# A token router run in batches of tiles behind its first stage, its rows stored from ACT's queue, and all eighteen weight chunks allowed early

## Chip, cores and metric

One core of one Trainium2 chip runs the whole program. The metric is the device time of one execution in microseconds (us). The program has two layers, and each ends in a mixture of experts (MoE) whose weights are streamed from HBM.

## The reference

Each layer normalises its tokens, runs four token mixers, projects their output with one 1024 x 1024 matrix, adds it to the stream with a gate, and then runs the MoE. Layer 0 has 768 tokens (512 latent, 256 context), the MoE of layer 1 only the 512 latent ones. The part around the change is this:

```
def moe_ffn(h, wg, bg, we, be, w_gate, w_up, w_down):
    lg = hf @ wg + bg                                  # 4 groups
    g_sel = argmax(lg); p_sel = softmax(lg)[g_sel]
    le_sel = (hf @ we + be).reshape(T, 4, 8)[g_sel]     # 8 experts of the group
    top_v, top_i = lax.top_k(le_sel, 2)
    wts = softmax(top_v) * p_sel
    ...
    y_e = (silu(x @ w_gate[e]) * (x @ w_up[e])) @ w_down[e]   # 32 experts, 1024 -> 512 -> 1024
    out[token] += wts * y_e
```

h is the normalised and modulated stream: x times its inverse root mean square (rs), times one row of factors, plus one row of offsets. Latent and context tokens have different rows.

## The kernel before

Tokens lie on partitions, 128 to a tile: 6 tiles in layer 0, 4 in layer 1. A scheduler orders the instructions of each engine by program order among those that it takes to be ready; what it has ordered, an engine runs strictly in turn.

**Output projection and first stage.** The last part of the projection (`c == 3`) makes a quarter of the columns of every tile: 24 matmuls on TensorE (PE, L1787), a product on VectorE (DVE, L1790) and an addition to `x1[t]` on GpSimd (POOL, L1791). `token_tile(t)` follows two tiles behind (`LAG = 2`): `x1[t]` is stored to `acc` (L1753), eight transposes go to PSUM (L1757), ScalarE (ACT) squares the tile and sums it (`row_rs`, L1170) and copies the transposes back (L1759), sixteen matmul passes give 36 logits (L1762). DVE makes rs by a Newton iteration (`small_rsqrt`, L1154 to L1162), the product of the row h2 (L1768), POOL adds the offsets (L1769), and h2 is stored to DRAM (L1770). For tiles 0 and 4 the two modulation rows and the gain are loaded and multiplied (L1764 to L1766); tile 4 is the first context tile and reuses their buffers. All these transfers are issued by SyncE's queue (SP). The buffer `h2` exists twice and also holds the gain.

**Router.** `rt.tile(t)` runs one tile behind that: three rounds of `first_max` (L891 to L894), softmax parts, two small matmuls that rank the tokens of an expert (L922, L923), the values EV (L932), the slots S (L936) and matmuls into the tables L (L937). `finish` turns L into gather and scatter indices (`table`, L956 to L970) and the counts of each expert.

**Weights.** An expert's weights are six chunks of 1 MB. There are 18 chunk slots, so three experts fit. `fetch(n)` issues the loads of chunks up to n on SP; at most five are on their way (`FLIGHT`), and a load waits until its slot is free. Four chunks (layer 0) or seven (layer 1) are loaded before the last part of the projection. The other slots lie over the projection's operands (freed by its last matmul) and over `x1` and the router's buffers. After the router `fetch(FIRST[l])` allows chunks up to 12 in layer 0 and 16 in layer 1; those up to 18 wait until the second gather has landed (L1109). A later chunk waits for PE to have read the chunk that lies in its slot.

**Experts.** POOL gathers an expert's tokens by index (L990), PE transposes them (L1000) and multiplies gate and up (L1012), then the hidden part is transposed (L1025) and multiplied down (L1039), and POOL adds the rows to `acc` by index (L1052). An expert with more than 64 tokens takes a second round.

## Time and profile before

| | us |
|---|---|
| median of 3 runs (lowest, highest) | 2423.11 (2415.92, 2425.83) |
| the profiled execution | 2419.79 |
| its span, first to last instruction | 2418.0 |
| layer 0: last projection matmuls start / first gather issued / first expert's transposes | 771.35 / 812.19 / 818.01 |
| layer 1: first stage of tile 1 on PE / first gather issued / first expert's transposes | 1873.32 / 1911.46 / 1916.62 |

The mean granted clock of PE is 0.956 of 2.4 GHz. Layer 0's experts lie in the long stretch of about 400 GB/s in the first half of the page, layer 1's in the one that ends the program. In a timeline a row is: start, duration, engine, line, operation, tiles, count, and in brackets the engine's idle time before it with what ended it. SPq is SP's queue, where a transfer's issue stands, not its landing. Times in a timeline are us from the first instruction; "mean" in a group by line is in ns.

### The profile page before, as it was taken

To read this page: it belongs to the slowest core of one execution; us is meant where nothing else is said; L and a number is where in the kernel's file an instruction comes from. 1 tells how busy PE (TensorE), PEld (TensorE's weight loads), DVE (VectorE), ACT (ScalarE), POOL (GpSimd) and SP (SyncE) were. 2 spreads that over 40 slices of the span, in tenths; PEclk is the share of its full clock that TensorE was granted. 3 is DMA by queue.
4 is the path that set the end of the run, shared out by engine and by line. 5 is a ranking of instruction groups with operands and counts; after the bars stand their busy time and mean duration, and the time that the engine had idled before them with its cause. 6 is when DMAs were issued, how large, how long until landed. Compare 5 with 4: busy or idle time off the path is not lost. (4 is left out here: it accounts for less than half of the span.)

```text
span 2418.0 us, 32200 instructions
## 1 busy us (share of the span) xinstructions
PE 2039.0 (84%) x11540; PEld 1186.2 (49%) x11540; DVE 999.4 (41%) x2435; ACT 573.2 (24%) x1138; POOL 537.2 (22%) x429
## 2 busy tenths in 40 slices
PE   5789999999999598887777598999899598877775
PEld 1458778766688333322222386686669333222221
DVE  6751865537746522221112437645584511111110
ACT  4433431344622100000000234314352100000000
POOL 1653413211013122211111225131102221111111
PEclk9999999999998699999999799999999699999998
DMA  6434524202244899999999425420233899999996
GB/s 242 165 116 176 194 105 147 81 9 69 85 143 142 299 378 387 405 401 404 400 395 411 173 92 175 147 103 18 86 126 133 313 393 410 409 408 409 410 403 258
DMA packets 139311, 581.54 MB, mean 241 GB/s; under 512 B 23984, under 2 KB 47873, under 8 KB 88630
## 3 DMA queue, kind: packets, MB, share of 16 engines
q1 hardware_dynamic: 124054, 555.89, 59.5%
q0 software_dynamic: 15008, 22.36, 3.9%
q8 instruction: 152, 2.49, 0.4%
q14 instruction: 97, 0.79, 0.1%
HBM read 554.17 MB, written 36.80 MB: 244 GB/s over the span
## 5 line engine op out<-in xcount | busy, mean ns | idle before, releaser
L1012 PE MATMUL pb<-side,arena 128*64 128x512 f32 x1224 | 288.9, 604 | 45.9 <-DMA side<-in_w_moe 42.2
L1016 DVE COPY arena<-pb 128x512 f32<-128x512 f32 x67 | 46.3, 691 | 501.5 <-PE pb L1012 501.5
L1012 PE MATMUL pb<-arena 128*64 128x512 f32 x920 | 217.9, 605 | 41.8 <-DMA arena<-in_w_moe 38.2
L1028 ACT ACTIVATE arena<-pb 128x256 f32<-128x256 f32 x67 | 25.7, 383 | 902.9 <-PE pb L1025 902.9
L1276 POOL TENSOR_TENSOR wl<-side,wh 128x1024 fp32r<-128x1024 f32 x52 | 125.4, 2412 | 395.5 <-ACT wh L1275 267.1
L1012 PEld LDWEIGHTS pb<-side,arena 128*64 128x64 f32 x1224 | 81.4, 137 | 246.5 <-issue 126.4
L1300 PE MATMUL pw<-hh,wh 128*128 128x512 f32 (+1 forms) x720 | 168.6, 366 | 3.1 <-DVE arena L495 1.9
L1300 PE MATMUL pw<-hh,wl 128*128 128x512 f32 (+1 forms) x720 | 160.5, 358 | 0.0
L1043 DVE SCALAR_TENSOR_TENSOR arena<-pb,arena 128x512 f32<-128x512 f32 x67 | 50.3, 750 | 263.2 <-PE pb L1039 254.5
L1039 PE MATMUL pb<-side,arena 128*64 128x512 f32 x576 | 137.8, 617 | 24.9 <-DVE arena L1029 20.4
L1300 PE MATMUL pw<-hl,wh 128*128 128x512 f32 (+1 forms) x720 | 158.2, 355 | 0.0
L1012 PEld LDWEIGHTS pb<-arena 128*64 128x64 f32 x920 | 62.2, 138 | 190.8 <-issue 96.0
L1052 POOL DMA_INDIRECT acc<-arena x35 | 55.2, 1577 | 387.8 <-DVE arena L1047 338.5
L1300 PEld LDWEIGHTS pw<-hh,wh 128*128 128x128 f32 x720 | 117.8, 190 | 36.1 <-issue 14.4
L1039 PE MATMUL pb<-arena 128*64 128x512 f32 x496 | 115.5, 599 | 21.3 <-DVE arena L1029 20.8
L1300 PEld LDWEIGHTS pw<-hh,wl 128*128 128x128 f32 x720 | 117.9, 189 | 25.1 <-issue 9.9
L1300 PEld LDWEIGHTS pw<-hl,wh 128*128 128x128 f32 x720 | 117.4, 189 | 24.4 <-issue 8.7
L1052 POOL DMA_INDIRECT out_dram<-arena x32 | 50.9, 1590 | 311.4 <-DVE arena L1043 297.2
L990 POOL DMA_INDIRECT arena<-h2d,arena x67 | 69.8, 1042 | 187.5 <-issue 56.0
L1791 POOL TENSOR_TENSOR arena<-arena 128x256 f32<-128x256 f32 x40 | 31.2, 782 | 292.2 <-DVE arena L1790 278.2
L1025 PE MATMUL pb<-ident,arena 128*128 128x128 f32 x268 | 42.4, 280 | 55.4 <-DVE arena L1016 55.4
L1039 PEld LDWEIGHTS pb<-side,arena 128*64 128x64 f32 x576 | 39.0, 140 | 101.5 <-issue 60.8
(367 smaller groups left out, 3444.2 us busy)
## 6 DMA issues: line engine op xcount, KB each, us to landing
side<-in_w_moe SPq DMA_DIRECT2D x215, 1024.0 KB
arena<-in_w_moe SPq DMA_DIRECT2D x169, 1024.0 KB
arena<-in_w_ada SPq DMA_DIRECT2D x53, 512.0 KB
side<-in_w_in SPq DMA_DIRECT2D x52, 512.0 KB
side<-in_w_ada SPq DMA_DIRECT2D x43, 512.0 KB
arena<-in_w_out SPq DMA_DIRECT2D x16, 512.0 KB
arena<-in_x SPq DMA_DIRECT2D x12, 512.0 KB
spd<-arena SPq DMA_DIRECT2D x23, 256.0 KB
```

What stands on the lines that cost most here:

```text
L990: E.gathered = nc.gpsimd.indirect_dma_start(out=xg, out_offset=None, in_=h2d, in_offset=bass.IndirectOffsetOnAxis(ap=gi, axis=0), **(dict( ...
L1012: nc.tensor.matmul(pg[64 * s:64 * s + 64], xT[:, j // 4, j % 4, :], W[j // 2][:, (j % 2) * 1024 + s * 512:(j % 2) * 1024 + s * 512 + 512], ...
L1016: nc.vector.tensor_copy(gu, pg)
L1025: nc.tensor.transpose(pt[:, c * 128:(c + 1) * 128], gu[:, c * 128:(c + 1) * 128], E.c["ident"])
L1028: nc.scalar.activation(hT, pv[:, :, 0, :], AF.Silu)
L1039: nc.tensor.matmul(pd[64 * s:64 * s + 64], hT[:, c, :], W[4 + c // 2][:, (c % 2) * 1024 + s * 512:(c % 2) * 1024 + s * 512 + 512], start=( ...
L1043: nc.vector.scalar_tensor_tensor(y, pd, w[0], g2[0], op0=ALU.mult, op1=ALU.mult)
L1052: E.nc.gpsimd.indirect_dma_start(out=acc, out_offset=bass.IndirectOffsetOnAxis(ap=si, axis=0), in_=y, in_offset=None, compute_op=ALU.add, ...
L1276: (nc.vector if k % 2 else nc.gpsimd).tensor_sub(lo, src, hi.bitcast(F32))
L1300: nc.tensor.matmul(ps[:, :n], w[:, j, :], h[:, j, a:a + n], start=(i == 0), stop=(i == 23))
L1791: nc.gpsimd.tensor_add(x1[t][:, cc], x1[t][:, cc], tmp)
```

## The change

The work of a token tile is cut in two. `token_tile(t, i)` keeps what needs no VectorE: the store of `x1[t]`, transposes, square, copy and logits, which now gather in one PSUM tile and one rs tile for a batch. A batch is tiles 0 to 3, and in layer 0 also tiles 4 and 5 (`BATCHES`). When the first stage of all tiles has been written down, `token_batch` makes rs, logits, modulation rows and h2 for a whole batch, and `rt.tiles` routes it: one instruction for up to four tiles where there was one for each. Operations that took a number for each partition as an operand become operations on two tensors, one of them broadcast. `finish` makes both tables at once. The stores of `x1` and h2 and the loads of the gain and the modulation rows move from SP's queue to ACT's. `FIRST` becomes 18 in both layers, so no chunk waits for a gather. The arena grows by 128 columns.

```diff
-FIRST = (12, 16)
+FIRST = (18, 18)
+BATCHES = (((0, 4), (4, 2)), ((0, 4),))
     def first_max(self, v, w, iota, tag):
         nc.vector.reduce_max(m, v, axis=AX)
-        nc.vector.scalar_tensor_tensor(e, v, m, iota, op0=ALU.is_equal, op1=ALU.mult)
+        nc.vector.tensor_tensor(e, v, wide(m), op=ALU.is_equal)
+        nc.vector.tensor_tensor(e, e, row, op=ALU.mult)
         nc.vector.tensor_reduce(i, e, axis=AX, op=ALU.min)
-        nc.vector.tensor_scalar(e, iota, i, None, op0=ALU.is_equal)
+        nc.vector.tensor_tensor(e, row, wide(i), op=ALU.is_equal)
-    def tile(self, t, lg):
+    def tiles(self, t0, lg):
...
+        nc.vector.tensor_sub(sm[:, 0], v2, v1)
+        nc.scalar.activation(sm[:, 0], sm[:, 0], AF.Exp)
         nc.vector.tensor_add(Ab, E1, E2)
+        for i in range(n):
+            nc.vector.tensor_add(self.seen[:, t0 + i + 1], self.seen[:, t0 + i], Ab[:, i])
+            nc.tensor.matmul(rk[:, i], E.c["before_b"], Ab[:, i], start=True, stop=False, skip_group_check=True)
+            nc.tensor.matmul(rk[:, i], E.c["ones_b"], self.seen[:, t0 + i], start=False, stop=True, skip_group_check=True)
...
+            nc.vector.tensor_tensor(self.EV[:, k, tt], bcast(Ek.unsqueeze(2), P, n, 6, 32),
+                                    bcast(v[:, k].unsqueeze(3), P, n, 6, 32), op=ALU.mult)
+        for k, Ek in enumerate((E1, E2)):
+            nc.vector.tensor_tensor(Ek, Ek, rk, op=ALU.mult)
+            nc.vector.tensor_reduce(self.R[:, k, tt], Ek, axis=AX, op=ALU.add)
+        nc.vector.tensor_scalar(R1, self.R[:, :, tt], -float(NSLOT), None, op0=ALU.add)
+        for k in range(2):
+            for b, R in enumerate((self.R[:, :, tt], R1)):
+                nc.vector.tensor_tensor(S, bcast(self.slots.unsqueeze(1), P, n, 128),
+                                        bcast(R[:, k].unsqueeze(2), P, n, 128), op=ALU.is_equal)
+                for i in range(n):
+                    nc.tensor.matmul(self.L[:, b * 512:b * 512 + 192], S[:, i],
+                                     self.EV[:, k, t0 + i].rearrange("p v e -> p (v e)"),
+                                     start=(t0 + i == 0 and k == 0), stop=(t0 + i == self.nt - 1 and k == 1),
+                                     skip_group_check=True)
-            def token_tile(t):
-                nc.sync.dma_start(half_rows(acc[l], t), x1[t])
+            def token_tile(t, i):
+                nc.scalar.dma_start(half_rows(acc[l], t), x1[t])
...
-                rs = row_rs(E, x1[t], "rs2")
+                lg, rs = batch[t - i]
+                nc.scalar.activation(E.t("xoj", DM, BF16, bufs=1), x1[t], AF.Square, accum_out=rs[:, i:i + 1])
                 nc.scalar.copy(hTt, pt.rearrange("p (j t) -> p j t", j=8))
                 for j in range(8):
+                    nc.tensor.matmul(lg[:, i], hTt[:, j], wa[v][:, j], start=(j == 0), stop=(j == 7),
+                                     skip_group_check=True)
+            def token_batch(t0, n):
+                nc.vector.tensor_scalar(rs, rs, 1.0 / DM, EPS, op0=ALU.mult, op1=ALU.add)
+                small_rsqrt(E, rs, "rs2", n)
+                nc.vector.tensor_tensor(lg, ps, bcast(rs.unsqueeze(2), P, n, 36), op=ALU.mult)
+                nc.vector.tensor_tensor(lg, lg, bcast(cb[v].unsqueeze(1), P, n, 36), op=ALU.add)
+                if t0 % 4 == 0:
+                    n2 = E.load("h2", d[f"n2g{l}"], bufs=2, queue=nc.scalar)
+                    mod[:] = [bc_row(v, 4, "rsc", 1, nc.scalar), bc_row(v, 3, "rsh", 1, nc.scalar)]
+                    nc.vector.scalar_tensor_tensor(mod[0], mod[0], 1.0, n2, op0=ALU.add, op1=ALU.mult)
+                for i in range(n):
+                    h2 = E.t("h2", DM, bufs=2)
+                    nc.vector.scalar_tensor_tensor(h2, x1[t0 + i], rs[:, i:i + 1], mod[0], op0=ALU.mult, op1=ALU.mult)
+                    nc.gpsimd.tensor_add(h2, h2, mod[1])
+                    nc.scalar.dma_start(half_rows(h2d[l], t0 + i), h2)
+                rt.tiles(t0, lg)
                     if c == 3 and t >= LAG:
-                        logits.append(token_tile(t - LAG))
-                        if t > LAG:
-                            rt.tile(t - LAG - 1, logits[t - LAG - 1])
-            rt.tile(nt - 1, logits[-1])
+                        t0, n = [b for b in batches if b[0] <= t - LAG][-1]
+                        token_tile(t - LAG, t - LAG - t0)
+            for t0, n in batches:
+                token_batch(t0, n)
```

## Rows read from the trace of the kernel before

**Rows 1.** The page's head: span, and GB/s in 40 equal slices

```profile
span 2418.0 us, 32200 instructions
...
GB/s 242 165 116 176 194 105 147 81 9 69 85 143 142 299 378 387 405 401 404 400 395 411 173 92 175 147 103 18 86 126 133 313 393 410 409 408 409 410 403 258
```

**Rows 2.** Windows, layer 0: busy us (instructions) by engine, PE clock, DMA share, GB/s

```profile
780.00:800.00 20.00, 12.72 (x65) 11.96 (x65) 17.54 (x94) 4.33 (x10) 4.68 (x2) 0.50 0.58 205
...
900.00:920.00 20.00, 18.39 (x90) 6.51 (x88) 3.90 (x6) 0.97 (x2) 2.64 (x2) 1.00 0.98 371
920.00:940.00 20.00, 17.69 (x88) 6.56 (x86) 5.55 (x9) 1.94 (x4) 4.20 (x3) 1.00 0.97 375
```

**Rows 3.** SP's waits (total, times, longest): 880:920, 920:960, 1920:2000

```profile
SPq L1378 <- PE pb L1012: 8.1, 4, 4.3
...
SPq L1378 <- PE pb L1039: 10.4, 4, 5.4
...
SPq L1378 <- PE pb L1012: 11.6, 8, 5.3
```

**Rows 4.** Timeline of SP's queue, layer 0, router

```profile
772.48 0.33 SPq L1378 DMA_DIRECT2D side<-in_w_moe  x1
...
776.56 1.21 SPq L1511 DMA_DIRECT2D arena<-modd  x2
...
798.92 0.32 SPq L1770 DMA_DIRECT2D h2d<-arena  x1
```

**Rows 5.** Timeline of POOL, both layers

```profile
757.03 2.37 POOL L1769 TENSOR_TENSOR arena<-arena 128x1024 f32<-128x1024 f32 x1 [2.13 <-DVE arena L1768]
...
812.19 1.25 POOL L990 DMA_INDIRECT arena<-h2d,arena  x1 [13.30 <-DVE arena L948]
...
1911.46 1.07 POOL L990 DMA_INDIRECT arena<-h2d,arena  x1 [18.84 <-DVE arena L964]
...
1963.38 1.61 POOL L1052 DMA_INDIRECT out_dram<-arena  x1 [7.35 <-DVE arena L1043]
...
1976.28 1.60 POOL L1052 DMA_INDIRECT out_dram<-arena  x1 [7.16 <-DVE arena L1043]
```

**Rows 6.** Timeline of PE, both layers, from projection to first expert

```profile
771.35 1.11 PE L1787 MATMUL pw<-woh,ol 128*128 128x256 f32 x8
...
796.70 0.18 PE L922 MATMUL pb<-arena,before_b 128*128 128x32 bf16 x1 [6.76 <-DVE arena L919]
...
818.01 1.09 PE L1000 MATMUL pb<-ident,arena 128*128 128x128 f32 x4 [8.17 <-DMA arena<-h2d,arena]
...
1873.32 1.03 PE L1757 MATMUL pa<-ident,arena 128*128 128x128 f32 x8
...
1896.54 3.63 PE L1762 MATMUL pb<-arena 128*128 128x36 f32 x16 [1.10 <-ACT arena L1759]
...
1916.62 1.12 PE L1000 MATMUL pb<-ident,arena 128*128 128x128 f32 x4 [7.45 <-DMA arena<-h2d,arena]
```

**Rows 7.** Groups by line (busy, mean ns, idle before), DVE and ACT, 745:815

```profile
L892 DVE SCALAR_TENSOR_TENSOR arena<-arena,miota 128x32 f32<-128x32 f32 (+1 forms) x18 | 9.1, 509 | 0.1
L1768 DVE SCALAR_TENSOR_TENSOR arena<-arena 128x1024 f32<-128x1024 f32 x6 | 7.7, 1280 | 0.2
...
L1790 DVE TENSOR_TENSOR arena<-pw,arena 128x256 f32<-128x256 f32 x6 | 2.5, 416 | 2.5 <-PE pw L1787 2.5
...
L1759 ACT COPY arena<-pa 128x1024 f32<-128x1024 f32 x6 | 6.0, 1005 | 5.3 <-PE pb L1762 3.9 <-PE pa L1757 1.3
```

**Rows 8.** Timeline of DVE, layer 0: beside a POOL addition, and two chained steps

```profile
757.35 2.07 DVE L892 SCALAR_TENSOR_TENSOR arena<-arena,miota 128x4 f32<-128x4 f32 x1
...
806.10 0.25 DVE L892 SCALAR_TENSOR_TENSOR arena<-arena,miota 128x32 f32<-128x32 f32 x1
806.38 0.19 DVE L893 TENSOR_REDUCE arena<-arena 128x1 f32<-128x32 f32 x1
```

**Rows 9.** The gathers' line: issue to landing, all 67 of both layers

```profile
DMA to landing us min/median/max: 3.6/7.5/10.4
```

More of the change, by code (lines that the diff above doesn't have):

```diff
@@ L886, in first_max @@
     def first_max(self, v, w, iota, tag):
-        E, nc = self.E, self.E.nc
-        m, i = E.t(tag + "m", 1, bufs=2), E.t(tag + "i", 1, bufs=2)
-        e = E.t(tag + "e", w, bufs=2)
+        E, nc, n = self.E, self.E.nc, v.shape[1]
+        m, i = E.t(tag + "m", 4, bufs=1)[:, :n], E.t(tag + "i", 4, bufs=1)[:, :n]
+        e = E.t(tag + "e", [4, w], bufs=1)[:, :n]
+        wide = lambda a: bcast(a.unsqueeze(2), P, n, w)
+        row = bcast(iota.unsqueeze(1), P, n, w)
         nc.vector.reduce_max(m, v, axis=AX)
-        nc.vector.scalar_tensor_tensor(e, v, m, iota, op0=ALU.is_equal, op1=ALU.mult)
+        nc.vector.tensor_tensor(e, v, wide(m), op=ALU.is_equal)
@@ L921, in tile @@
-        rk = E.p1()[:, :32]
-        nc.tensor.matmul(rk, E.c["before_b"], Ab, start=True, stop=False, skip_group_check=True)
-        nc.tensor.matmul(rk, E.c["ones_b"], self.seen[:, t], start=False, stop=True, skip_group_check=True)
-        v = self.vals[:, :, t]
+        nc.vector.tensor_sub(sm[:, 0], v2, v1)
+        nc.scalar.activation(sm[:, 0], sm[:, 0], AF.Exp)
+        Ab = E.t("rA", [4, 32], BF16, bufs=1)[:, :n]
+        nc.vector.tensor_add(Ab, E1, E2)
+        rk = E.p1()[:, :n * 32].rearrange("p (n e) -> p n e", e=32)
@@ L925, in tile @@
+        w = sm[:, 2:4]
+        nc.vector.reciprocal(w[:, 0], sm[:, 1])
+        nc.vector.tensor_mul(w[:, 1], w[:, 0], sm[:, 0])
+        v = self.vals[:, :, tt]
         for part in range(3):
-            nc.vector.tensor_copy(v[:, :, 2 + part], w)
+            nc.vector.tensor_copy(v[:, :, :, 2 + part], w)
             if part < 2:
-                nc.vector.tensor_sub(w, w, v[:, :, 2 + part])
-        tmp = E.t("rtmp", 32, bufs=2)
+                nc.vector.tensor_sub(w, w, v[:, :, :, 2 + part])
@@ L930, in tile @@
         for k, Ek in enumerate((E1, E2)):
-            R, EV = self.R[:, k, t:t + 1], self.EV[:, k, t]
-            nc.vector.tensor_tensor(EV, bcast(Ek.unsqueeze(1), P, 6, 32), bcast(v[:, k].unsqueeze(2), P, 6, 32), op=ALU.mult)
-            nc.vector.tensor_tensor_reduce(tmp, Ek, rk, 1.0, 0.0, op0=ALU.mult, op1=ALU.add, accum_out=R)
-            for b in range(2):
-                S = E.t("rS", 128, BF16, bufs=4)
-                nc.vector.tensor_scalar(S, self.slots, float(b * NSLOT), R, op0=ALU.add, op1=ALU.is_equal)
-                nc.tensor.matmul(self.L[:, b * 512:b * 512 + 192], S, EV.rearrange("p v e -> p (v e)"),
-                                 start=(t == 0 and k == 0), stop=(t == self.nt - 1 and k == 1), skip_group_check=True)
+            nc.vector.tensor_tensor(self.EV[:, k, tt], bcast(Ek.unsqueeze(2), P, n, 6, 32),
+                                    bcast(v[:, k].unsqueeze(3), P, n, 6, 32), op=ALU.mult)
@@ L940, in finish @@
     def finish(self):
         E, nc = self.E, self.E.nc
-        tables = [self.table(self.L[:, b * 512:b * 512 + 192], 32, self.keep, f"s{b}") for b in range(2)]
+        gi, si, w = self.table(self.L.rearrange("p (b c) -> p b c", b=2)[:, :, :192], 2, 32, self.keep, "s")
         c = E.p1()[:, :32]
@@ L1761, in token_tile @@
                 for j in range(8):
-                    nc.tensor.matmul(ps[:, :36], hTt[:, j], wa[v][:, j], start=(j == 0), stop=(j == 7))
-                if t % 4 == 0:
-                    n2 = E.load("h2", d[f"n2g{l}"], bufs=2)
-                    mod[:] = [bc_row(v, 4, "rsc", 1), bc_row(v, 3, "rsh", 1)]
-                    nc.vector.scalar_tensor_tensor(mod[0], mod[0], 1.0, n2, op0=ALU.add, op1=ALU.mult)
-                h2 = E.t("h2", DM, bufs=2)
-                nc.vector.scalar_tensor_tensor(h2, x1[t], rs, mod[0], op0=ALU.mult, op1=ALU.mult)
@@ L1769, in token_tile @@
[L1769 to L1775 removed]
+                    nc.tensor.matmul(lg[:, i], hTt[:, j], wa[v][:, j], start=(j == 0), stop=(j == 7),
+                                     skip_group_check=True)
+            def token_batch(t0, n):
+                v = t0 // 4
+                ps, rs = (a[:, :n] for a in batch[t0])
+                nc.vector.tensor_scalar(rs, rs, 1.0 / DM, EPS, op0=ALU.mult, op1=ALU.add)
+                small_rsqrt(E, rs, "rs2", n)
+                lg = E.t("rlg", [4, 36], bufs=1)[:, :n]
+                nc.vector.tensor_tensor(lg, ps, bcast(rs.unsqueeze(2), P, n, 36), op=ALU.mult)
[3 more added lines that the diff above has]
+                    mod[:] = [bc_row(v, 4, "rsc", 1, nc.scalar), bc_row(v, 3, "rsh", 1, nc.scalar)]
+                    nc.vector.scalar_tensor_tensor(mod[0], mod[0], 1.0, n2, op0=ALU.add, op1=ALU.mult)
+                for i in range(n):
[4 more added lines that the diff above has]
+                rt.tiles(t0, lg)
@@ L1776, in trunk @@
+            mod, batch = [], {}
+            batches = BATCHES[l]
             for c in range(4):
```

83 lines of the change are left out of this document (35 added, 48 removed).

## The prediction

> **What bounds the kernel now.** Read first the page's head: both expert stages run at about 400 GB/s, and the five slices before the first one rises, with attention, projection and router, lie at 9 to 143 [rows 1]. A chunk of 1 MB (1.049 MB in the page's unit) takes 1.049/0.405 = 2.6 us at such a rate, so an expert's six take 15.6 us of transfer. It is tempting to say that whatever fills the empty slices earlier comes off the end. The windows at the start of the experts speak against that: in layer 0 the share of the DMA engines is 0.98 and 0.97 and the rate 371 and 375 GB/s between 900 and 940 [rows 2], and SP's waits say why: there it waits for PE to have read a slot, 8.1 us in four waits, then 10.4 in four; in layer 1 11.6 us in eight [rows 3]. PE takes an expert in 1976.28 - 1963.38 = 12.9 us [rows 5], faster than the transfers, but it starts with three experts in the slots and everything behind them waits for it. So the transfers catch up with PE early in both layers, and what they were ahead before that is lost. From there the end moves with the moment at which PE starts the first expert, almost one for one: 818.01 and 1916.62 [rows 6].
>
> That moment is set by the router. The first gather is issued at 812.19 and 1911.46, in both layers after a long idle time of POOL that ended with the router's tables on DVE [rows 5]. In layer 0 DVE is busy 17.54 of 20 us with 94 instructions [rows 2], and PE stands 6.76 us in front of a ranking matmul that waits for DVE, with the logits of the last tile behind it [rows 6]. So I ask of each part of the change what it does to the two first gathers.
>
> **First stage.** No router matmul now stands between the tiles' first stages. On PE a tile's projection is 24 matmuls at 1.11/8 us less their overlap, some 2.9 us. Before, the last eight started at 771.35 and ended at 772.5 [rows 6]; without the router's waits I take some 767.5. A tile's first stage after that is transposes 1.03 (1.0), copy 1.0 [rows 6, 7] and logits of about half of the 3.63 us that they take at half clock, 1.9: 4 us, since one PSUM buffer makes them follow each other. Layer 0: the logits of tile 3 at 771.5, of tile 5 at 779.5. Layer 1: tile 1 starts at 1873.32, three tiles later it is 1885.3, or 1889.6 if the clock falls for most of it (in 780 to 800 the granted clock is 0.50, the 1.2 GHz level, with PE waiting [rows 2, 6]); I take 1887.5, where the last logits before started at 1896.54 [rows 6].
>
> **The chain of a batch.** The price of a DVE instruction from two rows: 256 columns 416 ns, 1024 columns 1280 [rows 7], so 0.13 us and 1.125 ns for each column. A step that depends on the one before it costs 0.03 more: 806.10 + 0.25, next at 806.38 [rows 8]; a small step is 0.22 (0.19 + 0.03). For four tiles: scaled logits 2 x 0.32; group maximum 5 x 0.22 and mask 0.22; masked logits 0.30; two maxima over 128 columns 2 x 5 x 0.30 and one mask 0.30; sum of both 0.30, running count 4 x 0.22; of nine weight steps five on the path, 1.1; EV of 768 columns 2 x 1.0; ranks 4 x 0.30 and 0.2; slots of 512 columns 4 x 0.73. Sum 14.2 us. Then the last matmuls into L 1.0, and table to gather index: a copy of 384 columns and three small steps, 1.4.
>
> Of instructions DVE loses more than half: before 47 a tile (11 ahead of the router, 36 in it), with 27 and 22 for modulation and tables 309 in layer 0 and 210 in layer 1; now 56 + 2n a batch of n, with 14 and 12 for the tables 138 and 76. But before they ran in two interleaved chains at (17.54 - 3 x 1.28 - 2.07)/90 = 0.13 us each [rows 2, 7, 8], while a lone batch pays the chained step and starts when its slowest tile has arrived.
>
> **Layer 0.** First batch 771.5 + 14.2 = 785.7. The second batch's 60 instructions fill the first one's gaps in part and the rest follows: 60 x 0.13 = 7.8. Modulation and two h2 products 3.8. The first batch's h2 I take as made before 771, since its squares need no later tile; of POOL's additions two lie over the chain and each holds one DVE instruction for 2.07 us [rows 5, 8]: 4.1. So 801.4, and with 2.4 for matmuls and table the gather at 803.8, against 812.19: 8.4 earlier. The last h2 store, before at 798.92, 22.4 us behind the loads for tile 4 [rows 4], falls within that if those are issued before some 780.
>
> **Layer 1.** 1887.5 + 14.2, one h2 product 1.3, two additions 4.1, matmuls and table 2.4: 1909.5 against 1911.46, 2 us earlier.
>
> **Gathers beside weights.** Before, the first gather took 818.01 - 812.19 = 5.8 and 5.2 us to PE's first transpose [rows 5, 6]. With FIRST at 18 the chunks whose slots lie over `x1` and the router's buffers are issued at about the moment of the gathers and not behind them. The price of a gather beside full weight traffic is between 3.6 and 10.4, median 7.5 [rows 9]; I take the median: 2 us later in each layer.
>
> **Queues.** SP no longer stands behind POOL for the stores, so chunk 4, issued at 772.48 [rows 4], starts some 5 us earlier and the ten chunks over the projection's operands follow without gaps. By the first part this is worth nothing: PE gives the slots back when it starts. ACT issues 18 (layer 0) and 11 transfers more, at 0.33 us each as on SP [rows 4]: 6 and 4 us on an engine that is busy 4.33 of 20 us in 780 to 800 [rows 2], nothing on the path unless a wait stands in front of a copy. What stands behind such a wait is the copy, and behind the copy PE's logits.
>
> **A rule that speaks against it.** A POOL addition of 2.37 us held one DVE instruction 2.07 us and the h2 products, of which none ran beside an addition, took 1.28 each [rows 5, 7, 8]; now the products of a batch follow each other, each beside the addition of the one before. Held like that instruction, two or three of them cost layer 1 some 5 us, one costs layer 0 some 2; since the products are ready early I leave this out of the sum and put it into the range. The Trainium skill, "SBUF — State Buffer", section "Who interferes with whom", says that a DVE instruction with two SBUF inputs is blocked for the whole of a GpSimd instruction that reads SBUF, and nearly all of the new chain has two. By that rule the upper end of those 5 and 2 us would be the sum.
>
> **Sum.** -8.4 + 2 and -2 + 2.3: -6.1, so 2419.8 becomes 2413.7 for an execution like the profiled one, which lies 3.3 under the median of the runs; as a median **2417 us**, 0.25% faster. About 0.5%, 12 us, is what a measurement of this kernel can tell from no change, so I forecast no measurable change.
>
> Ends. Layer 0: no addition in the way, -4.1, no slower gather, -2; second batch wholly behind the first, 60 x 0.22 in place of 0.13, +5.4, gather 10.4, +2.9, blocked products +2. That is -12.5 to +4. Layer 1: full clock -2.2, no additions -4.1, gather as before -2.3; half clock +2.1, gather +2.9, blocked products +5: -8.3 to +10. Together -21 to +14, as medians 2402 to 2437.
>
> **Rivals.**
> *The count of instructions decides (27%).* If fewer instructions simply mean a shorter router, the second batch hides wholly in the first one's gaps (-7.8) and no addition holds DVE (-4.1 in each layer): -6.1 - 16 = -22.1, a median of 2401. For it: 171 and 134 fewer instructions and a DVE that is nearly full in 780 to 800. Against: they cost 0.13 us there, not their whole duration, and the batch's wide ones are longer. The Trainium skill, "VectorE: DVE Perf Modes", section "The TRN2 errata", says that an instruction with its source in SBUF pays a fixed extra time and advises wide ones; it points the same way.
>
> *The early chunks decide (8%).* If the expert stage were bound by transfers from its first chunk, eight chunks ahead in layer 0 and three in layer 1 would give 11 x 2.6 = 29 us: 2394. Against it speak SP's waits for PE.
>
> *The batch waits for its slowest tile (18%).* ACT is in order: if the square of tile 3 comes behind the copies of tiles 1 and 2, no rs exists before 771, DVE and POOL have nothing to do until then, and everything stands in a row behind the last logits. Layer 0: 771.5 + 7 wide products 8.9 + six additions that hold DVE 12.4 + 14.2 + 60 x 0.22 + 2.4 = 822.6; layer 1: 1887.5 + 5.1 + 8.3 + 14.2 + 2.4 = 1917.5. With the gathers +12.4 and +8.4: 2444, slower by 0.86%. It decides from a first h2 product that starts after some 768 in layer 0; for it speaks that the store of `x1`, the square and the copy of a tile stand together in ACT's program, against it that tile 3's `x1` is whole long before its transposes.
>
> **Chances.** Forecast 47%; faster by over 0.5%: 27 + 8 = 35%; slower 18%. The range from 2398 to 2437 takes in both ends above and the first rival; it leaves out the early chunks and the worse half of the slow case, about 2 in 10. The forecast alone is 2411 to 2430.
>
> **What the profile after would show.** Right: the last projection matmul near 767.5 with no ranking matmul before the last logits; DVE's count in the router halved; the first gathers at about 804 and 1909; the first transposes 7 to 8 us behind them; SP waiting for PE right after. Wrong: a gather before 798 or behind 812; an ACT wait for an h2 buffer in front of a copy; a first gather of 10 us or more; an end that moves other than by the two starts of the first expert.

## The result, and the profile after

The changed kernel takes 2430.1 us (median of 11 runs), the kernel before, run beside it on the same chip, 2415.9: ratio 1.0058, 95% interval 1.0045 to 1.0071. That is slower by 0.58%, where the forecast was 0.25% faster. The 2423.1 at the head of this document was a median of three runs; over eleven it is 2415.9, and the profiled execution of before lies 3.9 over that. The profiled execution has a span of 2429.2 us, 11.2 over that of before [rows 1].

First the stations. The transposes of the first token tile, in layer 0 and in layer 1, give a zero mark for the router of each layer. These are PE's rows before:

```profile
750.28 1.03 PE L1757 MATMUL pa<-ident,arena 128*128 128x128 f32 x8
...
1867.61 1.03 PE L1757 MATMUL pa<-ident,arena 128*128 128x128 f32 x8
```

The same on PE's timeline after, with the first transposes of an expert behind them, and POOL's two first gathers:

```profile
752.30 1.03 PE L1764 MATMUL pa<-ident,arena 128*128 128x128 f32 x8
...
831.94 1.08 PE L1016 MATMUL pb<-ident,arena 128*128 128x128 f32 x4 [9.72 <-DMA arena<-h2d,arena]
...
1878.05 1.03 PE L1764 MATMUL pa<-ident,arena 128*128 128x128 f32 x8
...
1927.72 1.12 PE L1016 MATMUL pb<-ident,arena 128*128 128x128 f32 x4 [7.68 <-DMA arena<-h2d,arena]
...
824.61 1.16 POOL L1006 DMA_INDIRECT arena<-h2d,arena  x1 [10.21 <-DVE arena L985]
...
1922.37 1.03 POOL L1006 DMA_INDIRECT arena<-h2d,arena  x1 [11.50 <-DMA arena<-in_w_moe]
```

The first gather of layer 0 comes 824.61 - 752.30 = 72.3 us behind the zero mark, before it was 812.19 - 750.28 = 61.9 [rows 5]: 10.4 lost. From the zero mark to PE's first expert it is 79.6 against 67.7. Layer 1 has 44.3 against 43.9 to the gather. PE's start of the first expert is 13.9 us late in layer 0 and 11.1 in layer 1, and the span 11.2. So nearly the whole loss of this execution is made in the router of layer 0, in the 55 us between the last projection product and the gather. DVE's timeline there, the long and the waiting instructions:

```profile
766.76 2.48 DVE L1789 SCALAR_TENSOR_TENSOR arena<-arena 128x1024 f32<-128x1024 f32 x2
776.03 0.31 DVE L1781 TENSOR_TENSOR arena<-pb,arena 128x144 f32<-128x144 f32 x1 [6.45 <-PE pb L1771]
781.74 1.28 DVE L1789 SCALAR_TENSOR_TENSOR arena<-arena 128x1024 f32<-128x1024 f32 x1 [5.41 <-DMA h2d<-arena]
783.48 2.00 DVE L894 TENSOR_TENSOR arena<-arena 128x16 f32<-128x16 f32 x1
...
806.09 1.23 DVE L1786 SCALAR_TENSOR_TENSOR arena<-arena 128x1024 f32<-128x1024 f32 x1 [4.20 <-DMA arena<-in_n2g]
...
809.82 2.36 DVE L915 SCALAR_TENSOR_TENSOR arena<-arena 128x64 f32<-128x64 f32 x1
...
812.47 2.01 DVE L894 TENSOR_TENSOR arena<-arena 128x64 f32<-128x64 f32 x1
```

A landing is the moment at which all data of a transfer have arrived. The first batch's third h2 product (781.74) waits for the landing of the first h2 store, since `h2` has two buffers; the first batch's chain stands behind it in DVE's order and has only begun at 783.48. The second batch's modulation product (806.09) waits for the gain row, and behind it stands what is left of the router. In these two waits DVE is idle for 5.41 and 4.20 us. ACT's queue and SP's queue show when these transfers were issued, and beside what:

```profile
771.49 0.33 ACTq L1791 DMA_DIRECT2D h2d<-arena  x1
...
781.12 4.69 ACTq L1791 DMA_DIRECT2D h2d<-arena  x2
...
794.60 0.33 ACTq L1791 DMA_DIRECT2D h2d<-arena  x1
795.02 0.51 ACTq L170 DMA_DIRECT2D arena<-in_n2g  x1
...
769.11 37.28 SPq L1384 DMA_DIRECT2D side<-in_w_moe  x10
...
848.73 0.34 SPq L1384 DMA_DIRECT2D arena<-in_w_moe  x1
```

A store of 0.5 MB takes 781.74 - 771.49 = 10.2 us and the gain row, issued 0.4 us behind a row store, 806.09 - 795.02 = 11.1, while ten weight chunks of 1 MB are issued on SP's queue from 769.11 to 806. What the early chunks gained is given back at 848.73, where SP has waited 14.1 us for PE to free a slot. A second thing is in the DVE rows: a step of 16 columns that takes 2.00 us, and others like it, beside POOL's additions. An instruction that is lengthened beside such an addition is called held below.

The first stage has waits of its own (ACT, PE and POOL in layer 0), and layer 1 has one landing in front of DVE:

```profile
771.91 1.01 ACT L1769 COPY arena<-pa 128x1024 f32<-128x1024 f32 x1 [4.55 <-POOL arena L1790]
...
772.98 3.01 PE L1771 MATMUL pb<-arena 128*128 128x36 f32 x16 [2.19 <-ACT arena L1769]
...
768.19 5.57 POOL L1790 TENSOR_TENSOR arena<-arena 128x1024 f32<-128x1024 f32 x2 [3.34 <-DVE arena L1789]
773.72 0.72 POOL L1811 TENSOR_TENSOR arena<-arena 128x256 f32<-128x256 f32 x1
...
1903.41 1.29 DVE L1789 SCALAR_TENSOR_TENSOR arena<-arena 128x1024 f32<-128x1024 f32 x1 [3.43 <-DMA h2d<-arena]
```

### The profile page after: what moved, and what is told of

Its sections match the earlier page's. It is cut to its first block, busy times and chain, and to the rows that moved or that the text cites. A ratio compares the mean times of both kernels' runs of the same rounds, so it can differ in the third digit from the quotient of the medians.

```text
span 2429.2 us, 31865 instructions
## 1 busy us (share of the span) xinstructions
PE 2032.2 (84%) x11540; PEld 1178.6 (49%) x11540; DVE 968.1 (40%) x2130; ACT 567.2 (23%) x1114; POOL 536.9 (22%) x429
```

## Experiments

The theory of landings: in this order DVE stands behind transfers of the router's own (row stores, then the second batch's gain and modulation rows), and beside the weight chunks these take 10 us and more. Its rivals are three. The batch's chain itself, or POOL's holds on it, may be what is long. Or it is ACT's queue, in which stores stand behind copies. Or it is the longer train of early chunks.

Executions shift as a whole before the token part begins. The zero mark of layer 0 lies between 744.89 and 758.86 us in these runs, but always 121.9 to 123.7 us behind the issue of the first weight chunk, except in u6 (below). So the gather is counted from the zero mark, "offset" below. An offset is read from one execution of each kernel. Each run is compared with the kernel before on its own chip; the medians of that kernel there were 2414.1, 2416.2, 2415.3, 2416.5 and 2416.3 us on the five chips.

| run | offset L0 | to expert | stage L0 | offset L1 | median us | ratio to before |
|---|---|---|---|---|---|---|
| before | 61.9 | 67.7 | 506.6 | 43.9 | 2415.9 | |
| changed | 72.3 | 79.6 | 505.9 | 44.3 | 2430.1 | 1.0058 (1.0045 to 1.0071) |
| u4 rows in place | 62.8 | 70.1 | 505.4 | 42.6 | 2419.7 | 1.0019 (1.0005 to 1.0032) |
| u5 chunks held | 64.2 | 74.3 | 522.6 | 40.8 | 2453.4 | 1.0174 (1.0150 to 1.0198) |
| u1 12 and 16 chunks | 71.5 | 76.6 | 506.6 | 44.8 | 2428.2 | 1.0061 (1.0044 to 1.0079) |
| u2 batches alone | 63.1 | 70.3 | 507.9 | 45.3 | 2430.0 | 1.0061 (1.0043 to 1.0080) |
| u6 in place, own rows | 58.1 | 65.6 | 505.8 | 40.9 | 2433.9 | 1.0084 (1.0064 to 1.0104) |
| u7 before, in place | 60.9 | 68.7 | 506.4 | 44.2 | 2413.5 | 1.0002 (0.9986 to 1.0019) |
| u8 in place, SP's queue | 66.3 | 73.6 | 506.2 | 41.0 | 2424.4 | 1.0037 (1.0018 to 1.0055) |
| u3 before, ACT's queue | 61.8 | 65.5 | 507.9 | 42.8 | 2416.3 | 1.0002 (0.9991 to 1.0014) |
| u9 in place, DVE adds | 65.0 | 72.6 | 506.4 | 43.3 | 2420.6 | 1.0025 (1.0007 to 1.0043) |
| u11 same, 12 and 16 | 65.7 | 71.8 | 504.8 | 41.1 | 2422.4 | 1.0023 (1.0008 to 1.0037) |
| u12 before, 18 and 18 | 60.4 | 67.6 | 507.9 | 43.9 | 2420.8 | 1.0023 (1.0008 to 1.0039) |
| u10 before, in place, DVE adds | 55.3 | 58.9 | 507.8 | 40.8 | 2406.9 | 0.9960 (0.9945 to 0.9975) |
| u13 u9, own scale row | 65.5 | 72.8 | 505.5 | 43.8 | 2428.4 | 1.0046 (1.0029 to 1.0062) |
| u14 before, DVE adds | 60.8 | 65.9 | 507.1 | 43.3 | 2410.1 | 0.9974 (0.9959 to 0.9989) |
| u15 u10, own scale row | 59.8 | 63.5 | 505.5 | 40.9 | 2409.7 | 0.9967 (0.9954 to 0.9981) |
| u16 u9, both rows early | 53.9 | 61.2 | 506.1 | 40.9 | 2412.2 | 0.9984 (0.9969 to 0.9998) |
| u17 u16, POOL adds | 58.6 | 65.9 | 507.9 | 43.2 | 2419.4 | 1.0021 (1.0004 to 1.0037) |

"To expert" is the offset of PE's first transpose of an expert, "stage L0" from there to the issue of the last weight chunk. The time does not follow the gather alone. From the first expert of layer 0 to the zero mark of layer 1, which holds the experts of one layer and the mixers of the next, these executions take 1042.8 (u15) to 1054.6 us (u6), and 1063.9 in u5. Differences of a few us in the time are therefore not read as effects of an edit where the intervals overlap.

**Rows in place (u4).** The product overwrites the token tile, whose store and transposes are done by then, so no product waits for a buffer.

```diff
-                    h2 = E.t("h2", DM, bufs=2)
+                    h2 = x1[t0 + i]
```

> The changed kernel with the rows h2 written over x1, so that no product waits for a buffer that a store still reads. Theory of landings (DVE, in its order, stands behind the landing of the first row store, which took 10 us beside the weight chunks): the third and fourth products of layer 0 follow the first two, before 780; the first batch's chain begins about 778 instead of 784; the first gather of layer 0 comes at 814 to 819 instead of 824.6, that of layer 1 two to four us earlier still against its stage, and the time is 6 to 12 us under the changed kernel's. Theory of the batch (the chain over all tiles, held by POOL and waiting for its last tile, is what is long): the first gather of layer 0 stays within 3 us of 824.6 and the time within 3 us of the changed kernel's.

DVE and POOL:

```profile
766.21 6.33 DVE L1789 SCALAR_TENSOR_TENSOR arena<-arena 128x1024 f32<-128x1024 f32 x2
...
773.53 2.01 DVE L894 TENSOR_TENSOR arena<-arena 128x16 f32<-128x16 f32 x1
...
811.76 1.16 POOL L1006 DMA_INDIRECT arena<-h2d,arena  x1 [11.02 <-DVE arena L985]
```

The third and fourth product follow at 766.21, the chain has begun by 773.53, the gather comes at 62.8: 9.5 us won, and 10 us of time with it, as the theory of landings said. The theory of the batch is out as the main cause. Yet the two products take 6.33 us where two alone take 2.48, and the kernel is still 0.19% over the one before.

**Chunks held (u5).** Nothing is taken from the code here but the traffic: the chunks wait for the last h2 store.

```diff
-                    nc.scalar.dma_start(half_rows(h2d[l], t0 + i), h2)
+                    stored[0] = nc.scalar.dma_start(half_rows(h2d[l], t0 + i), h2)
...
-            wts.fetch(FIRST[l])
+            wts.fetch(FIRST[l], stored[0])
```

> The changed kernel with the weight chunks from the fifth on held until the last h2 row of the layer is in memory, so that the router's own transfers have the DMA engines to themselves. Theory of landings: a row store takes about 3 us instead of 10, the third product starts by 777, the gain for the second batch lands 3 us behind its issue, and the first gather of layer 0 comes at 808 to 816. What the end does is open: 14 chunks start some 35 us later, and if the expert stage can't make that up the time is 10 to 25 us over the changed kernel's; if it can, 8 to 14 under. Theory of the batch: the first gather stays behind 820. Theory of ACT's order (stores stand behind copies of transposes): the stores still wait for the copy of tile 5's transposes, and the first gather comes at 817 to 822.

ACT's queue and DVE:

```profile
767.37 0.33 ACTq L1791 DMA_DIRECT2D h2d<-arena  x1
...
772.48 1.27 DVE L1789 SCALAR_TENSOR_TENSOR arena<-arena 128x1024 f32<-128x1024 f32 x1
...
777.34 0.81 ACTq L1791 DMA_DIRECT2D h2d<-arena  x2
```

The store that took 10.2 us has landed within 5.1, and the gather comes at 64.2, 8.1 earlier, though store and product are as in the changed kernel. So the landing is long because of the chunks. The gather lies just behind the range of that theory (816 is 63.7 behind the changed kernel's zero mark) and close to that of ACT's order (from 64.7), and the second and third store (777.34) did wait behind a copy here too: some of the loss may be that order's. The end is 23 us worse: the expert stage grows from 505.9 to 522.6 us in layer 0. More head start than before is worth nothing, but losing fourteen chunks of it is not made up.

**Batches alone (u2) and 12 and 16 chunks (u1).** Both have the lines below. In u2 all transfers that the change moved to `nc.scalar` go back to `nc.sync` as well, so u1 and u2 differ in the queue of the rows alone.

```diff
-FIRST = (18, 18)
+FIRST = (12, 16)
```

> The batches alone: rows, gain and modulation go through SP's queue again, ahead of the weight chunks there, and 12 and 16 chunks are allowed early, as before the change. Theory of landings: with no side chunk ahead of the third store the third product starts by 777 and the first gather of layer 0 comes at 806 to 815; time 2408 to 2420 where the kernel before has 2416. Theory of the batch: first gather of layer 0 behind 820, time 2425 to 2433.

> The changed kernel with 12 and 16 instead of 18 weight chunks allowed ahead of the first gather (that part undone). Theory of landings: the first eight chunks run beside the first stores as before, so the third product still waits until about 781; only the second batch's loads (issued 792 to 795) meet fewer chunks; first gather of layer 0 two to five us earlier than 824.6, time 1 to 5 us under the changed kernel's. Rival (the longer train of early chunks is the whole loss): first gather at 812 to 815, time 9 to 13 us under. Rival (the head start is worth something): time over the changed kernel's by 3 us or more.

The first h2 store and the third product, in u1 and then in u2:

```profile
766.79 0.33 ACTq L1791 DMA_DIRECT2D h2d<-arena  x1
...
776.46 1.28 DVE L1789 SCALAR_TENSOR_TENSOR arena<-arena 128x1024 f32<-128x1024 f32 x1 [4.86 <-DMA h2d<-arena]
...
774.04 0.32 SPq L1791 DMA_DIRECT2D h2d<-arena  x1
...
777.97 1.27 DVE L1789 SCALAR_TENSOR_TENSOR arena<-arena 128x1024 f32<-128x1024 f32 x1
```

u2's gather stands at 821.95, which taken as it stands is the figure of the theory of the batch (behind 820), and so is its median of 2430.0 (2425 to 2433). But this execution is late as a whole, its zero mark at 758.86. Counted from there the gather comes at 63.1, at the end of the other range (to 62.7), and the store lands within 3.9 us where u1's takes 9.7: on SP the chunks stand behind the stores, on ACT's queue they run beside them. So with two row buffers the move to ACT's queue costs 71.5 - 63.1 = 8.4 us at the gather. The time of u2 is not what the theory of landings says; it is that of the changed kernel. Its profiled execution, the slowest of its six, lost 2.6 us against the kernel before from the zero mark to the first expert in layer 0, 3.7 in layer 1, and 5.6 from there to the end. Whether the others lost the same is not shown, so the time stays open. u1 moved the gather by 0.8, less than any of its figures, and the time not by more than the runs scatter (1.0061 against 1.0058): the longer train of chunks is not the loss.

**The queue (u3, u8).** u3 moves only the row stores of the kernel before to ACT; u8 is u2 with the rows in place.

```diff
-                nc.sync.dma_start(half_rows(h2d[l], t), h2)
+                nc.scalar.dma_start(half_rows(h2d[l], t), h2)
```

> The kernel before with only the row stores (x1 and h2) moved to ACT's queue; gain and modulation rows stay on SP, chunks as before. Theory of landings: the chunks are no longer behind the stores on SP and run beside them, so the stores take about 10 us, and with two buffers for h2 every product stands behind the store two tiles back: first gather of layer 0 at 64 to 72 us behind the first transposes instead of 61.9, time 2 to 10 us over the kernel before. Rival (queue choice costs nothing, as the prediction had it): within 1 us of 61.9 and within 3 us of the kernel before.

> Batches and rows in place, with rows, gain and modulation through SP's queue and 12 and 16 chunks early as before the change: against the run of rows in place through ACT's queue this shows what the queue and the early chunks are worth. If landings were the whole trouble: gather of layer 0 within 2 us of 62.8 behind the first transposes and the time within 3 us of 2419.7. If ACT's queue costs by its order (stores behind copies): gather 2 to 5 us earlier. If the chunks behind the stores on SP come too late: the expert stages are 3 us or more longer than 506 and 470.

u3 is the kernel before to 0.1%: the queue costs nothing tile by tile, and the theory of landings was wrong to expect a loss there. The third product starts 15.6 us behind the issue of the first store (775.66 and 760.10), so it has no landing to wait for, and SP, which stands behind the gain load here, issues only two chunks before 787. u8 is 5 us over u4, with intervals that overlap, and the gather 3.5 later, which none of the three expected. So with no product behind a store, ACT's queue is not the trouble either.

**The kernel before in place (u7).** The edit of u4.

> The kernel before with the rows h2 written over x1, nothing else. If the landing of stores holds the tile-by-tile order too: first gather of layer 0 at 55 to 59 us behind the first token tile's transposes instead of 61.9, and 3 to 7 us less in all. Rival (only the batches stand behind a store's landing, since tile by tile the stores come far enough apart): within 1.5 us of 61.9, and the time within 3 us of the kernel before.

60.9 and no difference: only the batches stand behind a store's landing.

**Own rows for the second batch (u6).** u4 with second buffers for the two modulation rows, and one chunk less ahead in layer 0 for the room.

```diff
-EARLY = ((0, 4), (2, 5))
+EARLY = ((0, 3), (2, 5))
...
-[bc_row(v, 4, "rsc", 1, nc.scalar), bc_row(v, 3, "rsh", 1, nc.scalar)]
+[bc_row(v, 4, "rsc", nv, nc.scalar), bc_row(v, 3, "rsh", nv, nc.scalar)]
```

> Rows in place as in the run before, and buffers of their own for the second batch's gain and modulation rows (room for them: three weight chunks instead of four ahead in layer 0), so that these loads wait for nothing of the first batch. Counted from the first token tile's transposes of layer 0, the first gather came 61.9 us later before the change, 72.3 after it, 62.8 with the rows in place. Theory of landings: the two rows of the second batch are made as soon as their logits are there, and the gather comes 54 to 59 us behind those transposes; time 4 to 8 us under that of rows in place alone, so 0 to 5 us under the kernel before. Rival (with the waits for landings gone, the chain of the batches itself, held by POOL, sets the gather): gather at 61 to 64, time within 2 us of rows in place alone. Rival (the chunk that is no longer loaded ahead is missed): first transposes of an expert later against the gather by 2 us or more.

The gather came at 58.1, inside the range. A window up to it (its length, busy us of PE, weight loads, DVE, ACT and POOL, then clock, DMA share, GB/s) shows DVE busy 39.33 of 40.90 us:

```profile
779.60:820.50 40.90, 18.08 (x105) 13.61 (x103) 39.33 (x123) 4.92 (x9) 16.12 (x7) 0.58 0.98 382
```

The time went up by 14 us over u4, where 4 to 8 less were expected, and the zero mark shows where: it is 133.5 us behind the first chunk's issue instead of 122.3. The modulation products, now early, stand ahead of projection work in DVE's order and wait 8.9 us for their gain rows, and PE stands 8.1 us behind that. Another 8 us went between the first expert of layer 0 and the zero mark of layer 1 (1054.6 against 1046.3); their cause is open.

**Additions on DVE (u9, u11, u10).** With no landing to wait for, DVE is full, and some 12 of its 45 us in u4 are instructions held beside a POOL addition. So the addition moves to DVE: in u9 on u4, in u10 on u7; u11 is u9 with 12 and 16 chunks.

```diff
-                    nc.gpsimd.tensor_add(h2, h2, mod[1])
+                    nc.vector.tensor_add(h2, h2, mod[1])
```

> Batches with the rows in place, and the modulation added to the h2 rows by DVE instead of POOL. With the landings gone DVE has no gap between the last projection product and the first gather of layer 0, and some 12 of its 45 us there are instructions that stand for about 2.1 us beyond their own time while POOL adds. Theory of the held DVE: six additions of 1.28 us (7.7) replace six holds of 2.0 to 2.2 (12), so the first gather of layer 0 comes 58 to 60 us behind the first token tile's transposes instead of 62.8, that of layer 1 at 39 to 41 instead of 42.6, and the time is 5 to 9 us under rows in place alone: 2411 to 2415. Rival (POOL's additions lie beside other waits and cost nothing): the additions lengthen DVE's chain, gather at 64 to 70, time 3 to 10 us over rows in place alone.

> The kernel before with rows in place and the modulation added by DVE, tile by tile as before. Theory of the held DVE: the tile-by-tile router is held as often (six additions, six holds of 2.1 to 2.3), so the gather of layer 0 comes at 55 to 58 us behind the first transposes instead of 60.9 and the time is 2 to 6 us under the kernel before. Rival (holds that fall into the projection are hidden under PE there, while additions on DVE delay the projection's own products): no gain, time within 3 us of the kernel before or over it.

> The same as batches with rows in place and additions on DVE, but 12 and 16 chunks early instead of 18. If the early chunks only slow the first gathers of rows: the step from the first gather to the first expert's transposes in layer 0 is 5 to 6 us instead of 7.3, time 1 to 3 us under its twin. If the head start is worth something: time over its twin by 2 us or more and longer expert stages.

u9 on ACT's queue and DVE:

```profile
773.93 2.42 ACTq L1791 DMA_DIRECT2D h2d<-arena  x4
780.07 2.34 ACTq L1517 DMA_DIRECT2D arena<-modd  x2
...
796.82 1.23 DVE L1786 SCALAR_TENSOR_TENSOR arena<-arena 128x1024 f32<-128x1024 f32 x1 [10.41 <-DMA arena<-modd]
```

The holds are gone and DVE now waits 10.41 us for the scale row, which lands 16.7 us after its issue, behind four row stores and beside the chunks. The gather at 65.0 is in the rival's range, but not for the rival's reason, and the time is 0.9 us over u4, in neither range: both expectations missed this landing. u11 differs from its twin by less than the runs tell. In u10, where the tiles come one by one, the same edit brings the gather to 55.3 and the time to 2406.9, 0.40% under the kernel before, more than the 2 to 6 us expected: the best version found, better than both kernels. DVE and POOL there, where the first row answers to the held one of before [rows 8]:

```profile
760.00 0.22 DVE L892 SCALAR_TENSOR_TENSOR arena<-arena,miota 128x4 f32<-128x4 f32 x1
...
809.50 1.16 POOL L990 DMA_INDIRECT arena<-h2d,arena  x1 [37.81 <-DVE arena L966]
```

**Early chunks in the kernel before (u12).**

```diff
-FIRST = (12, 16)
+FIRST = (18, 18)
```

> The kernel before with 18 chunks allowed early in both layers, nothing else. The prediction has this at nothing, since the transfers have caught up with PE by 900 us either way: within 3 us of the kernel before, expert stages of 505 to 508 and 469 to 472 us. Rival (the head start counts): 3 us or more faster with shorter expert stages. Rival (chunks beside the router's stores): gather of layer 0 two us or more later than 61.9 behind the first transposes and slower.

The stages keep their length (507.9, and in layer 1 470.6 against 470.3), so the head start is worth nothing. The kernel is 0.23% slower, 5.5 us where at most 3 were expected, though its gather came no later (60.4); of that the profile shows 3 us in layer 1 between the first gather and the first expert, 8.3 against 5.2.

**What is left of u10's gain (u14, u15).** u14 is the kernel before with the additions alone, u15 is u10 with a second buffer for the scale row.

> The kernel before with the modulation added by DVE and its two row buffers kept. Theory of holds: rows in place alone gave nothing, so the additions give all: gather of layer 0 at 54 to 58 us behind the first transposes, time 2403 to 2411. Rival (both are needed: without POOL's additions the stores come earlier and the products then stand behind their landing): gather at 58 to 62, time 2411 to 2417.

> The kernel before with rows in place, additions on DVE and a second buffer for the scale row. Theory of landings: tile by tile DVE has other work until the modulation row lands, so little is to be had: gather of layer 0 at 53 to 56 instead of 55.3, time within 3 us of 2406.9. Rival (the row's landing is a wait of this order too): 3 us or more under 2406.9.

Both are faster than before by 0.3%; their intervals overlap u10's, so whether the rows in place add to it, or the own row takes away, stays open. The gathers do not settle it: u14's, at 60.8, is in the rival's range while its time is in that of the holds, and u15's, at 59.8, is later than expected. The clock differs between these three executions: in the ten us from 20 behind the zero mark PE was granted 0.75 in u10, 0.52 in u15 and 0.50 in u14. The last logits end at 43.0, 46.7 and 48.1, and the gather follows 12 to 13 us behind them.

**The batches with nothing to wait for (u13, u16, u17).** u13 gives the scale row a buffer. u16 also puts the second shift row into the buffer of a projection row that is no longer read, so both load early in the room that was there; u17 is u16 with POOL's additions. The lines of u16:

```diff
-    n2 = E.load("h2", d[f"n2g{l}"], bufs=2, queue=nc.scalar)
-    mod[:] = [bc_row(v, 4, "rsc", 1, nc.scalar), bc_row(v, 3, "rsh", 1, nc.scalar)]
+    n2 = E.load("h2", d[f"n2g{l}"], bufs=1, queue=nc.scalar)
+    mod[:] = [bc_row(v, 4, "rsc", 2, nc.scalar), bc_row(v, 3, ("rsh", "g1")[v], 1 + v, nc.scalar)]
```

> Batches with rows in place and additions on DVE as two runs ago, and a second buffer for the scale row, so that only the shift row of the second batch is still loaded late; the chunks ahead and the room taken stay as they were. Theory of landings and holds (the batch's chain itself is short): DVE's wait of 10.4 us for the modulation row goes, the first gather of layer 0 comes 53 to 57 us behind the first token tile's transposes instead of 65.0, and the time is 6 to 11 us under that twin: 2409 to 2415. Rival (the chain over all tiles is slow in itself): the gather stays behind 60 and the time within 4 us of 2420. Rival (the shift row is now what is waited for): an idle time of DVE of 4 us or more in front of an addition of the second batch, gather at 58 to 62.

> Batches with rows in place, additions on DVE, and both modulation rows of the second batch loaded before their time (scale in a second buffer, shift in the buffer of a projection row that is no longer read). Theory of landings and holds (the chain of the batches is not slow in itself): no idle time of DVE in front of a landing, first gather of layer 0 at 50 to 54 us behind the first token tile's transposes (65.5 less 12.7 is 52.8), near the 51.5 that the prediction's sum gave (803.8 against 752.3); time 2406 to 2416. Rival (the chain itself is slow): gather at 58 or later.

> The same with the additions on POOL, as in the change. Theory of holds: six holds of 2.0 to 2.2 us in place of six additions of 1.25, so the gather comes 4 to 6 us later than in its twin, at 55 to 59 us, and the time is 3 to 7 us over the twin's. Rival (the holds are covered): gather within 2 us of the twin's.

u13 on ACT's queue and DVE, its wait now at the shift row, 20.7 us after the issue and behind four row stores:

```profile
773.46 2.42 ACTq L1791 DMA_DIRECT2D h2d<-arena  x4
775.95 0.44 ACTq L1517 DMA_DIRECT2D arena<-modd  x1
...
796.65 1.22 DVE L1790 TENSOR_TENSOR arena<-arena 128x1024 f32<-128x1024 f32 x1 [12.66 <-DMA arena<-modd]
```

The wait is the one that its last rival named, but the gather, at 65.5, lies behind that rival's range. The time, 8 us over u9 with intervals that overlap, is in no range.

u16, a step that was held in u4 and is not here, the gather, and the groups of the six products and the six additions (busy us, mean ns, idle time before):

```profile
776.78 0.17 DVE L894 TENSOR_TENSOR arena<-arena 128x16 f32<-128x16 f32 x1
...
803.42 1.16 POOL L1006 DMA_INDIRECT arena<-h2d,arena  x1 [34.87 <-DVE arena L985]
...
L1789 DVE SCALAR_TENSOR_TENSOR arena<-arena 128x1024 f32<-128x1024 f32 x6 | 7.5, 1280 | 0.0
L1790 DVE TENSOR_TENSOR arena<-arena 128x1024 f32<-128x1024 f32 x6 | 7.2, 1214 | 0.0
```

u17, the group of its six products, DVE beside POOL's additions, and the gather:

```profile
L1789 DVE SCALAR_TENSOR_TENSOR arena<-arena 128x1024 f32<-128x1024 f32 x6 | 10.6, 1785 | 0.0
...
781.36 0.82 DVE L1782 TENSOR_TENSOR arena<-arena 128x144 f32<-128x144 f32 x1
...
782.42 2.00 DVE L894 TENSOR_TENSOR arena<-arena 128x16 f32<-128x16 f32 x1
784.46 2.29 DVE L895 TENSOR_TENSOR arena<-arena,miota 128x16 f32<-128x16 f32 x1
...
795.30 2.11 DVE L894 TENSOR_TENSOR arena<-arena 128x8 f32<-128x8 f32 x1
797.42 2.30 DVE L927 SCALAR_TENSOR_TENSOR arena<-arena 128x4 f32<-128x4 f32 x1
...
816.45 1.16 POOL L1006 DMA_INDIRECT arena<-h2d,arena  x1 [16.75 <-DVE arena L985]
```

u16's gather at 53.9 is in the range of the theory, its time 18 us under the changed kernel's and 0.16% under the kernel before. u17 is 4.7 us later at the gather and 7 us in time: the price of the holds net of the additions. Against u10, tile by tile with the same additions on DVE, the batches of u16 gain 1.4 us at the gather, but PE's first expert starts 2.3 later (61.2 against 58.9) and the time is no better (0.9984 against 0.9960): no run here shows that the shorter count of instructions is worth anything.

## Why the prediction was wrong

The failed step is in its sum for layer 0: "The first batch's h2 I take as made before 771". Two of the four were (766.76); the third stood behind a store's landing until 781.74, the chain behind it, and the second batch behind the landing of its gain row. The sum had no term for a transfer that DVE waits for, and its price of the holds, the second step that failed, is too small. By its own terms, as offsets:

- **Gather of layer 0.** Predicted 803.8 - 750.3 = 53.5, measured 72.3, a miss of 18.8. Taking the landings away and leaving POOL's additions (u17) gives 58.6: the landings are 13.7 of it. DVE's two waits alone are 9.6 (5.41 and 4.20); that the rest is work of the second batch which no longer fills gaps of the first is argued, not shown.
- **Holds.** The sum has two holds, 4.1 us, in layer 0. In u17 the h2 products take 3.0 us too long (six at 1785 ns in place of 1280), the step behind them 0.5 (0.82 in place of 0.30) and four small steps 8.0 (the last four DVE rows of u17 above, less 0.17 each), 11.5 together: the term is 7.4 short. The prediction left blocked products out of the sum and in the range. The rule cited there (the Trainium skill, "SBUF — State Buffer", section "Who interferes with whom") agrees with these rows. The 16-column step with two SBUF inputs takes 2.00 us beside an addition and 0.17 without one.
- **The chain.** u16 less its six additions (three of 1.22, one of 1.20 and a pair of 2.35, 7.2 together) is 46.7, against 53.5 - 4.1 = 49.4 in the sum: the steps were priced about 3 us too high. So -3 + 7 + 14 = 18 of the 18.8.
- **Layer 1.** Predicted 41.9, measured 44.3, although the logits of tile 3 ended at 18.3 where the sum has 19.9. DVE stood 3.43 us for the landing of a store (1903.41). u16 has 40.9 with neither landing nor hold. The clock moves this offset as much: u9 and u13 do the same as u16 in layer 1 and have 43.3 and 43.8. In the ten us from 10 behind the zero mark they were granted 0.51 and 0.50, u16 0.77 and the changed kernel 0.76, and their logits of tile 3 end at 20.6 and 21.1 against 18.2 in u16. A single batch loads its rows in time, so no load stands in front of DVE behind the zero mark there.
- **First stage.** The projection as predicted: its last matmuls start at 768.56, 766.5 without the drift of 2.0, and no ranking matmul stands before the last logits. The logits not: those of tile 3 end at 23.7 and those of tile 5 at 33.5, where the sum has 21.2 and 29.2. ACT's idle time of 4.55 us ends with the POOL addition whose row it stores at 771.49; the copy of tile 3's transposes, which PE began at 768.88, runs behind that store at 771.91, and PE stood 2.19 us for it. The last addition to tile 5 (773.72) stood behind two h2 additions on POOL. DVE waited 6.45 us for tile 3's logits (776.03), but since the third product waited for its landing until 781.74, this lies under it.
- **Gathers beside weights.** Predicted 2 us later in each layer: 1.5 in layer 0 (7.3 against 5.8), 0.2 in layer 1.
- **Head start worthless, the end follows PE's start.** Right: the stages are 505.9 and 470.5 us against 506.6 and 470.3. u5 bounds it: it holds for chunks beyond those that the kernel before had. In that kernel they cost 0.23% (u12).
- **Queues.** Right for the order of before (u3), wrong for the batches with two row buffers: u1 and u2, which differ in the queue alone, have the gather at 71.5 and 63.1. The text gave the freed chunks a price on the gathers and none on the rows beside them. And the second store, whose row POOL had finished at 773.8, was issued at 781.12 behind a copy: the text saw only the copy that could wait for a store (as tile 3's did), not the store that waits for a copy.
- **Rivals.** None of them is what happened. "The batch waits for its slowest tile" came near the time of the gather (822.6) and had the six holds, but its condition, a first product after 768, was not met. The count of instructions decided nothing: DVE runs 305 fewer and waits.

## What to carry to other kernels

When work is gathered into a batch, each instruction in the strict order of its engine inherits every wait in front of it: list the buffers that the batch reuses and the loads that its second half needs, and price each landing beside whatever bulk transfer the change releases at the same time. A wait taken away is found again at the next late transfer (stores, then the scale row, then the shift row), so part of the gain shows only when the last is gone (72.3, then 62.8, 65.0, 65.5 and 53.9 in the changed kernel, u4, u9, u13 and u16). An addition "given away" to POOL can cost DVE more than doing it: here 1.9 us of hold (11.5 for six, u17) against 1.2 (7.2 for six, u16).

## What was not expected of the hardware

A 0.5 MB row transfer beside one stream of 1 MB chunks took 10.2 us, a second with a row store issued just ahead of it 11.1, and one behind four others 20.7, although rows and chunks were on different queues. The same store took at most 5.1 us with the chunks held, and 3.9 with the chunks behind it on its own queue (u2). A small step held on DVE lasts 2.0 to 2.4 us whatever its size, for 4 columns as for 64, beside additions of about 2.4 [rows 5]. In a batch of dependent steps there is one to hold for nearly every addition: in u17 six additions held four small steps and lengthened the products by 3.0 us.
